# All loads of the modulation weights ahead, the first head in halves, the context last

## The chip, the core and the metric

The kernel runs on one core of one Trainium2 chip. The metric is the device time of one execution in microseconds (us), lower is better. The engines are PE (TensorE, matrix products; PEld is its weight load), DVE (VectorE), ACT (ScalarE), POOL (GpSimd) and SP (SyncE, which here issues nearly all DMAs from one queue in order).

## What is computed

One layer of a diffusion backbone on 1024 latent tokens and 256 context tokens of width 1024, all in float32. Cut to the part that the change touches:

```python
shift, scale, gate = split(silu(c) @ w_mod + b_mod, 3)       # w_mod: 1024 x 3072
hc = rmsnorm(ctx, norm_g) * (1 + scale_c) + shift_c          # the same w_mod, with c_ctx
hx = rmsnorm(x, norm_g) * (1 + scale_x) + shift_x
q, k, v, lr_f, lr_b, ... = split(h @ w_in, ...)              # 4 heads, 128 keys, 256 values
la = log_sigmoid(lr @ w_gate_up + b) / 16                    # a decay per direction
s_f, s_b = final states of the gated linear attention over the context
o = gated linear attention over the latents, both directions, starting from s_f and s_b
```

Behind it come a pooling branch, two sets of gates, two branch projections, an output projection, the residual and a last RMS norm. The change leaves all of these alone.

## The kernel before, in words

Activations are kept transposed, as h^T: eight row tiles of 128 features (kt = 0 to 7; 0 to 3 is the first row half, 4 to 7 the second) by two halves of 512 tokens. To keep float32 accuracy at the faster matrix rate, an operand is split into a rounded part and a rest (`split`, L82: one copy on ACT, one subtraction on DVE), and a product W^T h becomes three products: hi hi, hi lo, lo hi.

The start goes as follows. Small vectors are loaded and turned into columns. **Modulation** (L201 to L236) has four parts b = 0 to 3: shift and scale of the first row half, then shift and scale of the second. Each has eight weight tiles of 128x512 (256 KB, tag `h`, 32 slots). For an even kt the float32 tile is multiplied whole (L214, which the trace shows as two instructions a tile); for an odd one it is split and multiplied twice (L216 to L219). A part ends with a copy of its PSUM row by ACT (tile `on`), four small transposes into bank `po` (L223) and two or three small DVE operations into `shA` or `sA` (L227 to L233). Between the weight tiles the ten token tiles of 512 KB are loaded and normalised (`load_x` and `normalise`, L118 to L133: two squares with sums on ACT, two small DVE operations, a power on POOL, two scalings on DVE): latent tiles 2 to 5 (first token half) during parts 0 and 1, the context's 0 and 1 and latent tiles 6 to 9 (second half) during parts 2 and 3. The low-rank weights are loaded at the start of part 2 (L136, one DMA of 128 KB and eight of 32 KB).

`latent_rows` and `context_rows` (L185, L192) make h^T: PE transposes four (or two) token blocks into a bank, ACT and DVE scale, shift and split it (`split_rows`, L174, banks `sc` and `pj` in turn). First half rows 0 to 3 follow part 1 (L236); the rest comes after part 3 (L594 to L599) in the order: latent rows 4 to 7 of the first token half, low-rank product 1, context rows, low-rank product 0, all rows of the second token half, low-rank product 2. Then `ctx_gates` (L322: decays of the context, through tile `xm` with the one slot of tag `bx`), the first head's keys (`head_k`), the context's keys with the same weights (`ctx_k`), queries (`head_q`), the decays of the latents (`gates`, L448, again in `bx`), values (`head_v`), the context's state for head 0, then for heads 1 to 3 (L608 to L610). After that four times `gla(h)` (scores and states) with the projections of head h + 1.

Program order is a priority and not the order on an engine: a planner places each instruction when, by its own model, its inputs, its slots and its engine are free, and among the ready ones takes the first in program order. Once planned, each engine's queue, SP's too, runs in that order. Every tag has a fixed number of slots (L37) and PSUM banks (L39: `pj` 3, `sc` 2, `o`, `st`, `tr` 1 each); a tile waits for a slot until the last reader of an earlier tile is done. Weights of `w_in` come as 512 KB through `wr` (2 slots) and are split into `wh` and `wl` (4 slots each).

Of the kernel before, what the change touches and what calls it, by code (L numbers as in the profile page):

```python
# [10 lines left out]
F32R = mybir.dt.float32r  # L11
# [4 lines left out]
P = 128  # L16
D = 1024
# [18 lines left out]
# slots of the one SBUF pool, by tag; PSUM banks, by tag  # L36
# [6 lines left out]
def hybrid_kernel(ctx: ExitStack, tc: tile.TileContext, x, ctx_in, rows, w_mod, b_gate_row,  # L43
# [35 lines left out]
    def load(out, in_):  # L79
        return nc.sync.dma_start(out=out, in_=in_)  # L80

    def split(hi, lo, src):  # L82
        """src = hi + lo, exactly, both float32r"""
        act(hi, src)
        tt(lo, src, hi.bitcast(F32), ALU.subtract)
# [4 lines left out]
    # ---- constants and small vectors as columns  # L90
# [20 lines left out]
    # ---- token tiles: load, root mean square, normalise  # L111
# [6 lines left out]
    def load_x(t):  # L118
        tag = "S0" if t < 2 else "v" if t < 6 else "qk"
        loaded.append(t)  # L120
# [14 lines left out]
    # ---- low-rank gate inputs, stacked parts on partitions  # L135
    def low_rank_weights():  # L136
        wraw = T("wr", [P, KT, 32])
# [8 lines left out]
        wup = T("wr", [P, HALF])  # L146
        for rep in range(4):
            load(wup[rep * 16:(rep + 1) * 16], w_up_f)
            load(wup[64 + rep * 16:64 + (rep + 1) * 16], w_up_b)
# [4 lines left out]
    # ---- modulation: shift and scale as columns [d, (latent, context)]  # L154
# [8 lines left out]
    def modulate(kt, t0, n, c, ptag):  # L163
        """psum of one row tile of xn^T and the scale and shift that make it h^T"""
# [9 lines left out]
    def split_rows(kt, t0, n, c, hi, lo):  # L174
        pt, sc_c, sh_c = modulate(kt, t0, n, c, ("sc", "pj")[kt % 2])
# [23 lines left out]
    token_tiles = [2, 3, 4, 5, 0, 1, 6, 7, 8, 9]  # L199
    loaded = []  # L200
    for b in range(4):  # L201
        s_, half_ = b % 2, b // 2
        c0 = s_ * D + half_ * HALF
        pm = PT("st" if b % 2 else "tr")
        if b == 2:
            wlr, wup_hi, wup_lo = low_rank_weights()
        for kt in range(KT):
            w = T("h", [P, HALF])
            load(w, w_mod[kt * P:(kt + 1) * P, c0:c0 + HALF])
            if kt % 2 == 1 and token_tiles and b * KT + kt in (1, 3, 5, 7, 17, 19, 21, 23, 25, 27):  # L210
                load_x(token_tiles.pop(0))
                normalise(loaded[-1])
            if kt % 2 == 0:
                mm(pm[:4], sil4[:, kt, :], w, kt == 0, kt == KT - 1)  # L214
                continue
# [3 lines left out]
            mm(pm[:4], cs4[:, kt, :], lo, False, kt == KT - 1)  # L219
        mrow = T("on", [4, HALF])  # L220
# [14 lines left out]
        if b == 1:  # L235
            latent_rows(0, range(4))  # L236
    for t in token_tiles:
        load_x(t)
    for t in token_tiles:
        normalise(t)  # L240

    # ---- weight stream: slots of 1024 columns, split into exact float32r parts
    ahead = [False]

    def wslot(src, shape, col_scale=None):
        """rows [p, k, n] of a weight; per k: (hi, lo)"""
# [18 lines left out]
    def wquad(w, c0, col_scale=None):  # L265
        """256 columns, all rows"""
# [6 lines left out]
    def proj_t(w, rhs_hi, rhs_lo, n):  # L273
        """psum[128 columns, n tokens] = W^T h"""
# [9 lines left out]
    def proj_n(w, lhs_hi, lhs_lo, tok):  # L284
        """psum[128 tokens, 256 columns] = h W"""
# [33 lines left out]
    # ---- context: final states of both directions  # L319
# [29 lines left out]
    def transpose_k(src, tag):  # L349
        """four of [dk, 128] -> [token, chunk, dk]"""  # L350
# [39 lines left out]
    # ---- latent heads  # L390
# [15 lines left out]
    def head_v(h, st):  # L406
        wv = weights_v(h)
        for t in range(8):
# [21 lines left out]
    # Queries and keys lie with their two decays side by side: slot 1 is what a left block gives to the  # L430
    # scores with its right neighbour (backward decay of queries, forward of keys), slot 0 is for right blocks.
    # Decays of tokens and blocks: array 0 has the backward one of the even and the forward one of the odd,
    # array 1 the others.
# [679 lines left out]
```

## Time and profile before

| what | value |
|---|---|
| device time, median of 3 runs | 1151.29 us (1150.8 to 1152.05) |
| span of the profiled execution | 1152.8 us |
| PE busy | 97% of the span |
| DVE, ACT busy | 70%, 43% |
| mean DMA rate | 120 GB/s |
| chain that ended last | PE 86%, DMA 6%, ACT 2%, DVE 2% |

The profiled execution has no time of its own beside its span; the span is 1.5 us above the median of the runs. The table says which engine is full on average. What the start of the kernel costs doesn't show in it, since the start is a twelfth of the span.

### The profile page before, as it was taken

The page shows a single profiled execution, that of the slowest core. Times are in us where ns is not written, and L with a number is a line of the kernel's source. Part 1 is how long each engine was busy: PE and PEld are TensorE (multiplying, and loading weights), DVE is VectorE, ACT ScalarE, POOL GpSimd, SP SyncE. Part 2 cuts the span into 40 slices and gives each one's busy share as a digit, 9 for nine tenths or more (in the row PEclk, how much of TensorE's full clock was granted, in tenths as well). Part 3 has the DMA queues.
Part 4 walks back from the last instruction along what each step waited for, and adds up shares of the span by engine and source line. Part 5 has one row for each costly group of instructions (what it writes and reads, how often), then busy time and mean ns, then how long its engine had stood idle before and what let it go on. Part 6 is the DMA issues. An engine that isn't in the chain of part 4 may idle for free.

```text
span 1152.8 us, 16292 instructions
## 1 busy us (share of the span) xinstructions
PE 1119.6 (97%) x5993; PEld 926.7 (80%) x5993; DVE 812.2 (70%) x1533; ACT 493.4 (43%) x962; POOL 24.2 (2%) x50
## 2 busy tenths in 40 slices
PE   6799999999999999999999999999999999999997
PEld 1268998798798798788888888888887886878997
DVE  4677458488588587698988867665768776757454
ACT  6697552462452552543333433343446324113233
POOL 0100000000000000100000000000000000000001
PEclk9899999999999999999999999999999999999999
DMA  8812150120220310103251463524448468982113
GB/s 292 291 37 74 42 151 28 56 73 20 65 65 20 85 44 20 55 28 119 82 161 50 128 201 119 167 84 129 151 137 269 161 197 287 298 302 94 38 38 146
DMA packets 119660, 138.40 MB, mean 120 GB/s; under 512 B 8803, under 2 KB 80669, under 8 KB 119454
## 3 DMA queue, kind: packets, MB, share of 16 engines
q1 hardware_dynamic: 119582, 137.38, 37.6%
q8 instruction: 47, 0.77, 0.3%
q14 instruction: 31, 0.25, 0.1%
HBM read 100.65 MB, written 32.51 MB: 116 GB/s over the span
## 4 chain that ended last, share of the span: by engine, by line
PE 86%; DMA 6%; ACT 2%; DVE 2%; issue 2%; SPq 1%; POOL 1%; POOLq 0%; ACTq 0%; DVEq 0%
PE ppj L77 59%; PE psc L77 19%; PE pst L77 3%; PE po L77 2%; DMA h<-w_mod 1%; DMA qk<-ga 1%; PE ptr L77 1%; DMA qk<-x 1%; DMA qk<-gb_T 1%; DMA wr<-w_in 1%; PE ptr L353 1%; ACT sw L63 1%; SPq L80 1%; DMA wr<-w_b 0%; DMA S<-ctx 0%
## 5 line engine op out<-in xcount | busy, mean ns | idle before, releaser
L77 PE MATMUL ppj<-h,wh 128*128 128x512 f32 x794 | 257.9, 401 | 1.0 <-ACT h L63 1.0
L63 ACT ACTIVATE wh<-wr 128x512 fp32r<-128x512 f32 (+1 forms) x183 | 113.7, 627 | 189.9 <-PE ppj L77 108.0
L77 PEld LDWEIGHTS ppj<-h,wh 128*128 128x128 f32 x794 | 146.8, 188 | 35.1 <-issue 2.9
L66 DVE TENSOR_TENSOR wl<-wr,wh 128x512 fp32r<-128x512 f32 (+1 forms) x183 | 124.8, 686 | 61.2 <-ACT wh L63 56.2
L77 PE MATMUL ppj<-wh,h 128*128 128x256 f32 x800 | 157.7, 283 | 0.0
L77 PE MATMUL ppj<-h,wl 128*128 128x512 f32 x397 | 157.2, 396 | 0.0
L77 PEld LDWEIGHTS ppj<-wh,h 128*128 128x128 f32 x800 | 129.9, 190 | 0.5 <-ACT qk L63 0.4
L77 PE MATMUL ppj<-wl,h 128*128 128x256 f32 x400 | 113.2, 283 | 0.0
L77 PEld LDWEIGHTS ppj<-h,wl 128*128 128x128 f32 x397 | 74.6, 188 | 15.1
L77 PEld LDWEIGHTS ppj<-wl,h 128*128 128x128 f32 x400 | 76.0, 190 | 0.2
L77 PEld LDWEIGHTS psc<-z,s 128*128 128x128 f32 x384 | 48.1, 188 | 9.8 <-issue 7.6
L487 DVE COPY_PREDICATED A<-msk,psc 128x512 f32<-128x512 uint8 x56 | 41.2, 735 | 19.8 <-PE psc L77 19.7
L77 PE MATMUL psc<-z,s 128*128 128x128 f32 x384 | 53.5, 280 | 0.0
L63 ACT ACTIVATE s<-s 128x512 f32<-128x512 f32 x60 | 36.9, 629 | 36.7 <-DVE s L66 31.6
L66 DVE TENSOR_TENSOR s<-s,ppj 128x512 f32<-128x512 f32 x60 | 40.7, 683 | 17.0 <-PE ppj L77 17.0
L63 ACT ACTIVATE s<-qk 128x256 f32<-128x256 f32 x56 | 23.1, 420 | 59.8 <-DVE qk L66 59.8
L74 DVE SCALAR_TENSOR_TENSOR S<-S,dec,pst 128x256 f32<-128x256 f32 x56 | 26.8, 478 | 26.3 <-PE pst L77 26.0
L77 PE MATMUL ppj<-S,wh 128*128 128x512 f32 (+1 forms) x132 | 41.2, 371 | 0.0
L77 PE MATMUL psc<-h,wh 128*128 128x512 f32 x126 | 39.1, 392 | 0.0
L66 DVE TENSOR_TENSOR s<-s,psc 128x512 f32<-128x512 f32 x43 | 29.2, 683 | 11.9 <-PE psc L77 10.2
L66 DVE TENSOR_TENSOR s<-s,bx 128x256 f32<-128x256 f32 (+1 forms) x64 | 30.5, 487 | 7.5 <-ACT bx L63 7.5
L66 DVE TENSOR_TENSOR on<-wr,wr 128x512 f32<-128x512 f32 x21 | 14.5, 691 | 30.0 <-DMA wr<-w_in 24.2
(518 smaller groups left out, 2390.3 us busy)
## 6 DMA issues: line engine op xcount, KB each, us to landing
wr<-w_in SPq DMA_DIRECT2D x65, 512.0 KB, 3.9
h<-w_mod SPq DMA_DIRECT2D x32, 256.0 KB, 5.4
qk<-sg SPq DMA_DIRECT2D x32, 256.0 KB, 5.3
sg<-s SPq DMA_DIRECT2D x28, 256.0 KB, 2.1
sw<-qk SPq DMA_DIRECT2D x64, 64.0 KB, 2.0
gb_T<-qk SPq DMA_DIRECT2D x16, 256.0 KB, 3.6
qk<-o SPq DMA_DIRECT2D x16, 256.0 KB, 4.7
ga<-s SPq DMA_DIRECT2D x16, 256.0 KB, 2.2
```

The costliest lines, as they stand in the source:

```text
L63: return nc.scalar.activation(out, in_, func, **kw)
L66: return nc.vector.tensor_tensor(out=out, in0=a, in1=b, op=op)
L74: return nc.vector.scalar_tensor_tensor(out=out, in0=a, scalar=s, in1=b, op0=op0, op1=op1)
L77: return nc.tensor.matmul(out, lhsT=lhsT, rhs=rhs, start=start, stop=stop)
L80: return nc.sync.dma_start(out=out, in_=in_)
L353: nc.tensor.transpose(pt[:, i * P:(i + 1) * P], src[i], ident)
L487: nc.vector.copy_predicated(A, msk[:, li:li + 1, :].to_broadcast([P, CPH, P]), chunks(pl))
```

## The change

All 32 modulation loads are issued ahead of the remaining token tiles, with the first head's key and query weights between them. Token tiles 6 to 9 follow them, and the context's two tiles come last. Parts 0 and 1 split two of eight weight tiles in place of four. The first head's keys and queries are multiplied for the first token half in two pieces, row tiles 0 to 3 and 4 to 7, in banks that stay open between; values of the first token half follow. Then come the second token half's rows, keys, queries and values, and after them the context: rows, low-rank product, keys, `ctx_gates`, and `gates(0)`. The head's key weights lie in the slot of tag `bx`, its query weights in four slots of `s2`. The low-rank up-weights are loaded by two DMAs in place of eight. Rows are made in banks `sc` alone. Comments are dropped too.

```diff
     def load_x(t):
-        tag = "S0" if t < 2 else "v" if t < 6 else "qk"
-        loaded.append(t)
+        tag = "S0" if t < 2 else "v" if t < 6 else "kt" if t == 6 else "S"
         src = ctx_in[t * P:(t + 1) * P] if t < 2 else x[(t - 2) * P:(t - 1) * P]
...
     def low_rank_weights():
-        wraw = T("wr", [P, KT, 32])
+        wraw = T("A", [P, KT, 32])
         load(wraw, w_in[:, O_LR:O_LR + 32].rearrange("(k p) n -> p k n", p=P))
...
-        wup = T("wr", [P, HALF])
-        for rep in range(4):
-            load(wup[rep * 16:(rep + 1) * 16], w_up_f)
-            load(wup[64 + rep * 16:64 + (rep + 1) * 16], w_up_b)
+        wup = T("sw", [P, HALF])
+        for d, src in enumerate((w_up_f, w_up_b)):
+            load(wup[64 * d:64 * d + 64],
+                 src.rearrange("(a r) n -> a r n", a=1).to_broadcast([4, 16, HALF]))
         wup_hi, wup_lo = T("lr", [P, HALF], F32R), T("lr", [P, HALF], F32R)
         split(wup_hi, wup_lo, wup)
...
     def split_rows(kt, t0, n, c, hi, lo):
-        pt, sc_c, sh_c = modulate(kt, t0, n, c, ("sc", "pj")[kt % 2])
+        pt, sc_c, sh_c = modulate(kt, t0, n, c, "sc")
         hf = T("s2", [P, n])
...
-    token_tiles = [2, 3, 4, 5, 0, 1, 6, 7, 8, 9]
-    loaded = []
-    for b in range(4):
-        s_, half_ = b % 2, b // 2
-        c0 = s_ * D + half_ * HALF
-        pm = PT("st" if b % 2 else "tr")
-        if b == 2:
-            wlr, wup_hi, wup_lo = low_rank_weights()
-        for kt in range(KT):
-            w = T("h", [P, HALF])
-            load(w, w_mod[kt * P:(kt + 1) * P, c0:c0 + HALF])
-            if kt % 2 == 1 and token_tiles and b * KT + kt in (1, 3, 5, 7, 17, 19, 21, 23, 25, 27):
-                load_x(token_tiles.pop(0))
-                normalise(loaded[-1])
-            if kt % 2 == 0:
+    def mod_load(b, kts):
+        c0 = (b % 2) * D + (b // 2) * HALF
+        ws = []
+        for kt in kts:
+            ws.append(T("h", [P, HALF]))
+            load(ws[-1], w_mod[kt * P:(kt + 1) * P, c0:c0 + HALF])
+        return ws
+
+    def mod_part(b, pm, ws, kts):
+        for w, kt in zip(ws, kts):
+            if kt % (4, 2)[b // 2] != (3, 1)[b // 2]:
                 mm(pm[:4], sil4[:, kt, :], w, kt == 0, kt == KT - 1)
                 continue
             hi, lo = T("wh", [P, HALF], F32R), T("wl", [P, HALF], F32R)
             split(hi, lo, w)
             mm(pm[:4], cs4[:, kt, :], hi, kt == 0, False)
             mm(pm[:4], cs4[:, kt, :], lo, False, kt == KT - 1)
+
+    def mod_finish(b, pm):
+        s_, half_ = b % 2, b // 2
...
-        if b == 1:
-            latent_rows(0, range(4))
-    for t in token_tiles:
-        load_x(t)
-    for t in token_tiles:
-        normalise(t)
+    x_after = {(0, 3): 2, (0, 7): 3, (1, 1): 4, (1, 4): 5}
+    for b in range(2):
+        pm = PT("st" if b % 2 else "tr")
+        for kt in range(KT):
+            ws = mod_load(b, [kt])
+            if (b, kt) in x_after:
+                load_x(x_after[b, kt])
+                normalise(x_after[b, kt])
+            mod_part(b, pm, ws, [kt])
+        mod_finish(b, pm)
...
-    def head_v(h, st):
-        wv = weights_v(h)
-        for t in range(8):
+    def head_v(h, st, hf=None, wv=None):
+        wv = wv or weights_v(h)
+        for t in range(8) if hf is None else range(hf * CPH, hf * CPH + CPH):
...
-    msk_f = T("bx", [P, len(LEVELS), P])
-    load(msk_f, masks)
-    nc.vector.tensor_copy(msk, msk_f)
+
+    def head_weights(c0, tiles):
+        raw = T("wr", [P, KT, P])
+        load(raw, wcols(w_in, c0))
+
+        def go():
+            for i in range(2):
+                split(*tiles[i], raw[:, 4 * i:4 * i + 4, :])
+            return [tuple(t[:, k, :] for t in tiles[i]) for i in range(2) for k in range(4)]
+        return go
+
+    def proj_part(pt, w, hf, kts):
+        for k in kts:
+            whi, wlo = w[k]
+            mm(pt, whi, hH[hf][k], k == 0, False)
+            mm(pt, whi, hL[hf][k], False, False)
+            mm(pt, wlo, hH[hf][k], False, k == KT - 1)
+
+    st = new_head()
+    kbig = T("bx", [P, 2, KT, P], F32R)
+    k_go = head_weights(O_K, [(kbig[:, 0, 4 * i:4 * i + 4], kbig[:, 1, 4 * i:4 * i + 4]) for i in range(2)])
+    ws2 = mod_load(2, range(KT))
+    q_go = head_weights(O_Q, [(T("s2", [P, 4, P], F32R), T("s2", [P, 4, P], F32R)) for i in range(2)])
+    ws3 = mod_load(3, range(KT))
+    wlr, wup_hi, wup_lo = low_rank_weights()
+    latent_rows(0, range(4))
+    pm2, pm3 = PT("tr"), PT("st")
+    mod_part(2, pm2, ws2[:4], range(4))
+    wk = k_go()
+    mod_part(2, pm2, ws2[4:], range(4, KT))
+    pk, pq = PT("pj"), PT("pj")
+    proj_part(pk, wk, 0, range(4))
+    mod_finish(2, pm2)
+    mod_part(3, pm3, ws3[:4], range(4))
+    wq = q_go()
+    mod_part(3, pm3, ws3[4:], range(4, KT))
+    mod_finish(3, pm3)
+    proj_part(pq, wq, 0, range(4))
+    for t in (6, 7, 8, 9):
+        load_x(t)
+    latent_rows(0, range(4, KT))
+    proj_part(pk, wk, 0, range(4, KT))
     rope_t = T("t8", [P, 2, L])
     load(rope_t, rope)
     cosT, sinT = rope_t[:, 0, :], rope_t[:, 1, :]
-    latent_rows(0, range(4, KT))
+    proj_part(pq, wq, 0, range(4, KT))
+    for t in (6, 7):
+        normalise(t)
+    st["k"][0] = rope_apply(pk, 0, 1.0)
+    wv = weights_v(0)
+    for t in (8, 9):
+        normalise(t)
+    st["q"][0] = rope_apply(pq, 0, float(P) ** -0.5)
+    head_v(0, st, 0, wv)
     low_rank(1, hH[0], hL[0])
+    latent_rows(1, range(0, KT))
+    for t in (0, 1):
+        load_x(t)
+    msk_f = T("z", [P, L + 2 * PAD])[:, :len(LEVELS) * P]
+    load(msk_f, masks.rearrange("p a b -> p (a b)"))
+    pk, pq = PT("pj"), PT("pj")
+    proj_part(pk, wk, 1, range(KT))
+    st["k"][1] = rope_apply(pk, 1, 1.0)
+    proj_part(pq, wq, 1, range(KT))
+    st["q"][1] = rope_apply(pq, 1, float(P) ** -0.5)
+    low_rank(2, hH[1], hL[1])
+    for t in (0, 1):
+        normalise(t)
+    head_v(0, st, 1, wv)
     context_rows()
     low_rank(0, hcH, hcL)
-    latent_rows(1, range(0, KT))
-    low_rank(2, hH[1], hL[1])
+    kc = ctx_k(wk)
     e_ctx = ctx_gates()
-    st = new_head()
-    wk = head_k(0, st)
-    kc = ctx_k(wk)
-    head_q(0, st)
+    nc.vector.tensor_copy(msk, chunks(msk_f))
     decays = gates(0)
-    wv = head_v(0, st)
     ctx_state(0, kc, ctx_v(wv))
```

## Rows read from the trace of the kernel before

**Rows 1.** The page, busy time of each engine over the whole span.
```profile
span 1152.8 us, 16292 instructions
PE 1119.6 (97%) x5993; PEld 926.7 (80%) x5993; DVE 812.2 (70%) x1533; ACT 493.4 (43%) x962; POOL 24.2 (2%) x50
```

**Rows 2.** Stretches: start:end, length, busy by engine (instructions), granted clock, DMA share, GB/s.
```profile
0.00:25.00 25.00, 17.97 (x57) 4.28 (x57) 10.77 (x30) 14.31 (x35) 2.53 (x9) 1.00 0.85 288
25.00:55.00 30.00, 20.53 (x64) 6.56 (x64) 18.21 (x48) 20.01 (x49) 3.29 (x6) 0.89 0.91 320
55.00:74.00 19.00, 16.83 (x87) 11.83 (x88) 17.61 (x33) 18.02 (x36) 0.00 (x0) 0.91 0.16 42
74.00:91.00 17.00, 16.88 (x71) 11.89 (x70) 11.34 (x25) 13.55 (x22) 0.10 (x1) 1.00 0.11 31
91.00:165.00 74.00, 73.75 (x544) 69.82 (x543) 42.65 (x97) 44.60 (x79) 0.10 (x1) 1.00 0.30 83
165.00:1152.80 987.80, 973.65 (x5177) 822.34 (x5175) 711.58 (x1302) 382.90 (x746) 18.23 (x33) 1.00 0.37 116
```

**Rows 3.** Instruction groups of PE, 0 to 90.9 us, three of 22.
```profile
L77 PE MATMUL ppj<-h,z 128*128 128x512 f32 x32 | 11.6, 468 | 1.7 <-ACT h L63 1.5 <-DVE h L66 0.2
L77 PE MATMUL ppj<-h,wh 128*128 128x512 f32 x32 | 11.4, 413 | 0.0
L77 PE MATMUL ptr<-h,sil 128*4 128x512 f32 x16 | 10.7, 759 | 2.4 <-ACT sil L63 2.4
```

**Rows 4.** The chain that ended last: start, length, engine and work.
```profile
66.25 0.44 PE psc L167 x4
73.25 0.43 PE po L77 x2
93.66 11.15 PE ppj L77 x50
105.93 29.16 PE ppj L77 x240
```

**Rows 5.** PE in order of time: start, length, work, [idle before, releaser].
```profile
20.20 1.02 PE L77 MATMUL pst<-h,sil 128*4 128x512 f32 x2
21.16 0.39 PE L77 MATMUL pst<-wh,cs 128*4 128x512 f32 x1
25.47 0.41 PE L223 MATMUL po<-cst,on 4*128 4x4 f32 x4 [0.68 <-ACT on L63]
...
38.96 1.87 PE L77 MATMUL ptr<-h,sil 128*4 128x512 f32 x2
...
53.27 0.41 PE L223 MATMUL po<-cst,on 4*128 4x4 f32 x4 [0.68 <-ACT on L63]
```

**Rows 6.** DMA view, 0 to 60 us, 40 slices of 1.5 us.
```profile
GB/s 0 145 299 320 275 272 403 407 393 389 382 389 388 327 142 79 307 273 359 347 406 380 396 389 389 384 396 374 395 418 421 362 296 254 44 0 0 0 0 0
```

**Rows 7.** ACT in order of time: first product split after the last load of part 1.
```profile
21.84 0.63 ACT L63 ACTIVATE wh<-h 128x512 fp32r<-128x512 f32 x1 [0.93 <-DMA h<-w_mod]
```

**Rows 8.** The chain that ended last, from the last modulation load on.
```profile
39.39 4.33 DMA h<-w_mod
43.73 0.61 ACT wh L63
...
48.58 0.56 POOL rstd L131
...
54.31 0.79 ACT h L63
```

**Rows 9.** From the context's rows to the first head's scores: PE, ACT and DVE in order of time.
```profile
55.81 0.48 PE L167 MATMUL ppj<-cst,S 128*128 128x128 f32 x1
...
70.04 0.50 PE L77 MATMUL po<-lr,lr 64*128 64x256 f32 x2
...
123.64 1.90 ACT L63 ACTIVATE bx<-bx 128x2032 f32<-128x2032 f32 x1 [2.12 <-DVE bx L66]
...
169.80 0.69 DVE L74 SCALAR_TENSOR_TENSOR A<-psc,cst 128x512 f32<-128x512 f32 x1
```

## The prediction, made before the change was run

> **What bounds the kernel now.** I read the page first: PE is busy for 97% of the span, no other engine for more than 70% [rows 1]. Then the stretches: from 91 us to the end PE is busy for 73.75 of 74.0 and 973.65 of 987.8 us, so it idles for 14 us in 1062 [rows 2]. From there on, whatever PE has done earlier comes off the end. Before 91 us PE looks busy as well, but its busy time misleads: it counts latencies and products at the lower clock. So I count its work instead, at the spacing that products show when they follow each other closely [rows 3 to 5]: 0.223 us for 512 columns (50 in 11.15 us), 0.1215 for 256 (240 in 29.16), 0.11 for a transpose, 0.215 for a gate product, 0.96 for a float32 modulation tile multiplied whole (20.20 to 21.16).
>
> By 90.9 us PE has done: 16 whole tiles 15.4; 32 products of split tiles 7.1; 32 low-rank products on latents 7.1 and 16 on context 1.9; 48 of the first keys 10.7; 80 transposes 8.8; 18 gate products 3.9; four ends of modulation parts 1.6. That is 56.5 us, so **34.4 of the first 90.9 us are lost to PE**. Of them 11.5 fall before 25 us (8 whole tiles, 16 products, 16 transposes and one end are 13.5). The other 22.9 come after it, and the chain says where: loads run at 380 to 400 GB/s [rows 6] and the last modulation tile lands at 43.7, but the first row that needs it starts at 54.3, since two tiles' normalisation, with a power on POOL in each, stands among the last splits on the in-order ACT and DVE [rows 8]. Then, from 55 to 74 us, DVE and ACT are busy for 17.6 and 18.0 of 19 us making rows [rows 2], while PE has only transposes and low-rank products. The first head, PE's bulk, begins at 74.
>
> **The change, part by part.** I ask when PE will have done the same work. Parts 0 and 1 multiply four more tiles whole and eight products fewer: +3.8 − 1.8 = +2.1 us (rounded), so the list is 58.6. The rest is the time that PE still loses, each term with both ends.
>
> a) Up to 25 us. Loads of parts 0 and 1 and tiles 2 to 5 are the same bytes, so the end of part 1 (25.47, [rows 5]) stays. The 2.1 us of more work fall partly into waits for loads. PE loses 11.5 now; I take 10 (10 to 12).
>
> b) Start of part 2. Its loads follow at once, PE has them while ACT and DVE make rows 0 to 3. 1 (0 to 2).
>
> c) End of part 3. Part 1's last tile landed at 21.8 [rows 7]. Behind it come the key weights, part 2, the query weights and part 3: 0.52 + 2.10 + 0.52 + 2.10 = 5.24 MB at 390 GB/s, 13.4 us, so part 3's last tile lands at 35.3, 8.4 us earlier than now. From the last load to the first row part 1 needs 4.7 us (21.84 to 25.47, and 1.04 more as from 53.27 to 54.31), part 3 now 10.6 (43.7 to 54.3) [rows 5, 7, 8]. With the normalisations behind it I expect the shorter way, so rows 4 to 7 start near 41. PE has 18.5 us to do between 25 and there: the two parts 11.3, 16 transposes 1.8, first pieces of keys and queries 5.4. It is covered nearly throughout. If the planner again puts tiles 6 to 9 among the last splits, ACT waits there for loads that land at 41 to 44. 3 (1 to 6).
>
> d) Values. Tiles 6 to 9, the rope table and the value weights are 4.2 MB behind part 3: 10.8 us, about 46 and with the low-rank loads 49; 53 if the context and the masks (1.5 MB) pass the value weights, which wait for both `wr` slots on SP with the rope exchanges queued behind them. PE's cover from 44.5 is the second pieces of keys and queries (5.4) and low-rank product 1 (3.6), to 53.5. 2 (0 to 4).
>
> The low-rank weights cause a dip to 142 and 79 GB/s at 19.5 to 24 us, worth 3.2 us of full rate [rows 6]. The change moves it behind part 3 and issues three DMAs for nine; I count 3 us before tiles 6 to 9, inside d. The Trainium skill (DMA: Bandwidth & Descriptors, Specifications) gives 512 bytes as the least transfer for line rate; the 128-byte rows of this load lie below it and the dip agrees. By it the dip would move whole and d would be 4: 1140 in place of 1138.
>
> e) Rows of the second token half. The same ACT and DVE work as now at 55 to 74, but PE has 23.3 us of values beside it, half of them without those rows. One pair of banks `sc` in place of five banks costs nothing while PE has that cover; without it I'd count 2 to 3 us. 2 (0 to 5).
>
> f) The context. Its rows, products and states move whole behind the head; PE has other work, so only hand-overs are lost. The key weights keep the `bx` slot until `ctx_k`; behind it wait `ctx_gates` and then `gates(0)` on ACT and DVE, and PE's scores wait for those. 1 (0 to 6; the far case is a rival).
>
> Everything else (the rope exchanges of the head's first half, earlier on SP; the mask's cast; the powers of four tiles on POOL) lies beside this cover and counts nothing; without it four powers at 0.56 us [rows 8] are 2.2 us.
>
> **Sum:** 10 + 1 + 3 + 2 + 2 + 1 = 19 us lost, with ends of 11 and 35. 58.6 + 19 = 77.6 us against 90.9: 13.3 us gained. The span goes from 1152.8 to 1139.5; the median of the runs is 1.5 us below the span, so **1138.0 us**. The ends give 1130 and 1154.
>
> **Rivals.** A measurement of this kernel tells 0.2%, 2.3 us, from no change.
>
> *All covered.* PE finds work at every hand-over: losses of 13, a gain of 19.3, 1132 us. For it: from 25 us on PE nearly always has two independent streams. Against: queues in order, planned on modelled times.
>
> *The lower clock.* The granted clock is 0.89 from 25 to 55 us and 0.91 from 55 to 74 [rows 2], and after 38 us a pair that takes 1.02 us takes 1.87 [rows 5], which is 1.2 for 2.4 GHz, in a stretch where PE is busy for 20.5 of 30 us. If half of the 18.5 to 19.4 us of work between 25 and 45 runs so, 9.5 us go: 1147.5. Against it: PE has less to wait for there. The Trainium skill (TensorE: Matmul & The Clock Gate, HAM oscillation) says that waits for loads between short groups of products make each group start at the low clock; the 1.87 us agree, and the loads still pace this stretch.
>
> *The context's chain ends up slower.* PE passes the values of the second half at 85 us of work (24.6 modulation, 1.6, 7.0, 7.1, 21.4 keys and queries, 23.3 values) plus 18 lost: 103. If the planner leaves the context's transposes till then, the chain from the first of them to the end of `gates(0)`, 55.81 to 125.54 now, 69.7 us [rows 9], ends at 173. PE's own work until then is 49 us, to 152: transposes 1.8, low-rank 1.9, gates 5.2, and for each of four heads keys 2.9, values 5.8 and a state 1.4. 20 us are open, which outweighs the gain: 1158. It decides once the gap exceeds 13 us and nothing fills it. Against it: head 1's projections (96 products of 512 columns and 192 of 256, 44.7 us) need nothing of that chain, the context's tiles are there at some 55 us, and scores on DVE start at 169.8 now, 44 us after the decays were ready [rows 9].
>
> *It doesn't do what it says.* The planner sorts by readiness and takes program order only among what is ready, so the queues may end up much as they are: 1151.
>
> **How the numbers follow.** Forecast 0.52, all covered 0.20, lower clock 0.10, context's chain 0.10, nothing 0.08. Faster by over 0.2% (below 1149): the first two and 0.07 of the third, 0.79. Within: 0.03 + 0.08 = 0.11. Slower: 0.10. The range 1129 to 1150 holds the first three, 0.82.
>
> **What would show it.** In the changed profile: the last modulation tile lands near 35 us and rows 4 to 7 start near 41 (c); the first product with value weights at 49 to 54 (d); PE idle below 3 us between 45 and 100; a granted clock of 1.00 from 25 us on, against the clock's rival. The first keys, low-rank products and both gates done would be 13 us earlier than at 90.9, and everything behind, such as the first scores' DVE operation at 169.8, earlier by about as much. Wrong I'd be if that operation isn't earlier while PE's products are: then the chain through `bx` bounds, and the gain is given back there.

## The result and the profile after

The changed kernel takes 1165.16 us, the median of 4 runs (1162.57 to 1168.17), beside 1151.67 us for the kernel before in 4 runs on the same chip. The ratio is 1.0111, with a 95% interval of 1.009 to 1.0133: **slower by 1.1%**, where 1.2% faster was forecast. The profiled execution is the slowest of the four: 1168.17 us, with a span of 1166.4.

The page of the kernel after, where [rows 1] show the kernel before:

```profile
span 1166.4 us, 16240 instructions
PE 1124.1 (96%) x5993; PEld 931.0 (80%) x5993; DVE 809.8 (69%) x1529; ACT 491.8 (42%) x958; POOL 24.2 (2%) x50
```

PE has as many instructions as before and is busy for 4.5 us more, while the span is 13.6 us longer. So most of the loss is time in which PE stands. The stretches of [rows 2], read again in the kernel after (start:end, length, busy by engine, granted clock, DMA share, GB/s), say where:

```profile
0.00:25.00 25.00, 18.59 (x51) 4.02 (x51) 9.12 (x27) 12.40 (x29) 2.53 (x9) 1.00 0.94 328
25.00:55.00 30.00, 20.83 (x64) 7.63 (x65) 15.17 (x35) 17.41 (x41) 1.65 (x3) 0.77 0.97 306
55.00:74.00 19.00, 18.63 (x121) 16.28 (x120) 11.85 (x30) 11.31 (x26) 1.64 (x3) 1.00 0.35 101
74.00:91.00 17.00, 15.72 (x95) 13.23 (x94) 11.01 (x16) 9.67 (x16) 0.00 (x0) 1.00 0.03 8
91.00:165.00 74.00, 66.36 (x447) 58.79 (x445) 39.75 (x81) 44.26 (x78) 0.20 (x2) 0.98 0.20 55
165.00:1166.00 1001.00, 984.00 (x5222) 831.04 (x5220) 722.92 (x1344) 396.79 (x771) 18.22 (x33) 1.00 0.36 115
```

In two places this isn't what was forecast. From 25 to 55 us PE is as little busy as before and its clock is 0.77 (0.89 before). From 91 to 165 us, where it idled for 0.25 us, it now idles for 7.6. From 55 to 74 us it is better: 121 instructions in place of 87.

Busy time counts waits for latency and the low clock as work, so I count PE's lost time as the prediction did: the length of a stretch less its instructions at full-rate spacing (0.223 us for 512 columns, 0.1215 for 256, 0.11 a transpose, 0.22 a gate product, 0.48 for each of the two instructions of a whole tile, 0.10 a small transpose). The stretches are cut at fixed times, and the runs that follow stand beside it. An instruction that lies across a cut counts on both sides, so that a count can come out a little below zero; it is good to about 1 us, and what is read from it is differences between kernels.

```
us lost to PE       0-25  25-55  55-74  74-113  113-200    sum
before              10.9   13.9    6.7     1.2      4.7   37.4
after                8.8   14.4    0.8     2.0     20.5   46.5
e1                   9.6   13.0    0.8     8.1     10.5   42.0
e2                   9.8    7.7    0.2     2.6     20.3   40.6
e3                  10.9   13.7    5.1    -0.6     23.4   52.5
e4                   9.2   10.1    0.7     2.7     21.7   44.4
e6                   9.7    6.2    6.2     2.9      9.3   34.3
e7                  10.9   12.7    9.6     2.8      4.7   40.7
e8                   8.9   14.0    0.9     1.9     12.2   37.9
e11                 10.9   13.0    4.2     3.3     11.6   42.9
```

The column 113-200, and with it the sum, is some 3 us too high in every row: products of the states (`pst<-S,on`, 256 columns) are counted at 0.1215 us, and follow each other in the trace at 0.215 (eight of them take 1.99 us). The differences stay.

To 200 us the change loses 46.5 − 37.4 = 9.1 us more, and does 2.1 us more work for its whole tiles: 11.2 us together. DVE's score operations show that this is nearly all of it. Its timeline before (the first such operation, at 169.80, is in [rows 9]) and after:

```profile
172.62 0.73 DVE L487 COPY_PREDICATED A<-msk,psc 128x512 f32<-128x512 uint8 x1 [2.13 <-PE psc L77]
...
190.38 0.68 DVE L74 SCALAR_TENSOR_TENSOR A<-psc,cst 128x512 f32<-128x512 f32 x1
```

```profile
158.86 0.68 DVE L74 SCALAR_TENSOR_TENSOR A<-psc,cst 128x512 f32<-128x512 f32 x1
...
182.26 0.73 DVE L490 COPY_PREDICATED A<-msk,psc 128x512 f32<-128x512 uint8 x1
...
200.45 0.68 DVE L74 SCALAR_TENSOR_TENSOR A<-psc,cst 128x512 f32<-128x512 f32 x1
```

The first score operation, which the prediction had named as its sign, comes 10.9 us earlier (158.86). It doesn't wait for the decays: it is done before `gates(0)` ends, at 179.9. The first masked one behind it (`COPY_PREDICATED`) starts 2.4 us after that end, where it started 47 us after it before, and it is 9.6 us later than before. The second score operation is 10.1 us later, the third goes from 255.50 to 266.65 (11.1 later), and POOL's memset of a tile `z` from 641.94 to 653.26 (11.3):

```profile
641.94 0.96 POOL L916 MEMSET z<- 128x1024 f32 x1 [57.36 <-DVE z L66]
```

```profile
653.26 0.96 POOL L974 MEMSET z<- 128x1024 f32 x1 [57.84 <-DVE z L66]
```

So most of the time is lost before some 200 us, and nearly nothing between there and 642. The last 2.3 us of the 13.6 come behind that: from 880 to 910 us the granted clock is 0.89 here, and 1.00 in the same work before (868.7 to 898.7). Of the traces below some have such a dip near 900 us and some don't. Of the two sides, up to 113 us the change wins 32.7 − 26.0 = 6.7 us, and from 113 to 200 it gives back 15.8.

**From 113 to 200 us.** What PE waits for there, in the view of its waits in the kernel after, 91 to 200 us (total, times, longest):

```profile
PE psc L77 <- DVE s L71: 3.4, 1, 3.4
PE pst L77 <- ACT on L63: 2.7, 2, 1.6
PE ppj L77 <- ACT S L63: 2.3, 1, 2.3
PE po L77 <- DVE bx L71: 0.9, 1, 0.9
```

At all four PE waits for ACT or DVE, for a step of one chain or for a copy (`S`, `on`) that stands behind such steps in ACT's queue. ACT's timeline shows the chain from end to end: the context's first row, a table load (`ACT_TABLE_LOAD`), the context's decays (`z`), the first decay of `gates(0)`, and its last exponential:

```profile
112.97 0.56 ACT L63 ACTIVATE S<-psc,shA,sA 128x256 fp32r<-128x256 f32 x1
...
129.55 1.28 ACT L63 ACT_TABLE_LOAD   x1
130.84 1.06 ACT L63 ACTIVATE z<-z 128x1024 f32<-128x1024 f32 x1
...
154.28 0.85 ACT L63 ACTIVATE bx<-psc,cols 128x256 f32<-128x256 f32 x2 [2.99 <-DVE z L319]
...
178.00 1.91 ACT L63 ACTIVATE bx<-bx 128x2032 f32<-128x2032 f32 x1 [0.83 <-DVE bx L66]
```

From 113.0 to 179.9 it takes 67 us (67.4 from the first transpose, at 112.5), against 69.7 before, from the first transpose at 55.8 to 125.5 [rows 9]. Seven table loads of 1.28 us stand in it on ACT in both kernels, 9 us of the 67. The chain is about as long as it was and begins 57 us later. What differs is what PE has beside it. The chain that ended last shows that it passes through ACT's and DVE's queues, among the splits of the context weights of other heads (the same view, 142 to 154 us):

```profile
142.04 0.36 ACT kt L63
142.41 0.52 ACT wh L63
142.93 0.36 ACT z L63
143.29 0.52 ACT wh L63
143.81 0.95 ACT z L63
...
151.41 0.69 DVE wl L66
152.10 2.16 DVE z L319 x6
```

**From 25 to 58 us.** The same view at the start, up to the last of part 3's products:

```profile
24.95 6.53 DMA h<-w_mod
...
32.24 8.75 DMA sw<-w_up_b
...
41.08 0.64 ACT lr L63
...
43.09 6.47 PE ptr L77 x13
...
51.31 3.57 PE pst L77 x10
```

ACT's timeline there:

```profile
41.08 0.63 ACT L63 ACTIVATE lr<-sw 128x512 fp32r<-128x512 f32 x1 [1.62 <-DMA sw<-w_up_b]
41.61 2.69 ACT L63 ACTIVATE wh<-h 128x512 fp32r<-128x512 f32 x5
...
57.71 0.78 ACT L63 ACTIVATE h<-psc,shA,sA 128x512 fp32r<-128x512 f32 x1
```

And PE's:

```profile
30.85 1.87 PE L77 MATMUL pst<-h,sil 128*4 128x512 f32 x2 [5.86 <-DMA h<-w_mod]
...
42.28 0.40 PE L77 MATMUL ptr<-wh,cs 128*4 128x512 f32 x1 [2.91 <-ACT wh L63]
```

Part 3's last load is issued at 30.15 us and lands 5.7 us later, at 35.9, so the weights are there when forecast (35.3). But ACT has the copy of the low-rank up-weights, which land at 41.0, ahead of the splits of parts 2 and 3, and five of these run in one go behind it. Before that, PE stands 5.86 us for a tile of part 3 that the planner put ahead of the rows' transposes, and ACT stands 6.43 us, to 34.34, for these transposes. Rows 4 to 7 start at 57.7 us: later than the 54.3 of before [rows 8], not earlier.

In the kernel before, the last load of part 3 is issued at 40.06 and lands at 45.7, not at 43.7 as the prediction read from [rows 8]. The split that starts at 43.7 had waited behind a copy of ACT, and this copy for PE, which was still at part 2:

```profile
43.24 0.59 ACT L63 ACTIVATE on<-ptr 4x512 f32<-4x512 f32 x1 [4.55 <-PE ptr L77]
```

### The profile page after: what moved, and what is told of

Its sections match the earlier page's. It is cut to its first block, busy times and chain, and to the rows that moved or that the text cites. A ratio compares the mean times of both kernels' runs of the same rounds, so it can differ in the third digit from the quotient of the medians.

```text
span 1166.4 us, 16240 instructions
## 1 busy us (share of the span) xinstructions
PE 1124.1 (96%) x5993; PEld 931.0 (80%) x5993; DVE 809.8 (69%) x1529; ACT 491.8 (42%) x958; POOL 24.2 (2%) x50
## 3 DMA queue, kind: packets, MB, share of 16 engines
q1 hardware_dynamic: 119462, 137.38, 36.9%
## 4 chain that ended last, share of the span: by engine, by line
PE 85%; DMA 6%; ACT 4%; DVE 2%; issue 1%; POOL 1%; SPq 0%; POOLq 0%; ACTq 0%; DVEq 0%
PE ppj L77 58%; PE psc L77 19%; PE pst L77 3%; PE po L77 2%; PE ptr L77 2%; DMA h<-w_mod 2%; DMA qk<-ga 1%; DMA qk<-gb_T 1%; DMA v<-x 1%; DMA sw<-w_up_b 1%; PE ptr L356 1%; ACT L63 1%; ACT wh L63 1%; DVE wl L66 1%; DMA wr<-w_b 0%
## 5 line engine op out<-in xcount | busy, mean ns | idle before, releaser
L77 PE MATMUL ppj<-h,wh 128*128 128x512 f32 x730 | 237.1, 401 | 1.0 <-ACT h L63 0.8
L63 ACT ACTIVATE wh<-wr 128x512 fp32r<-128x512 f32 x178 | 109.9, 627 | 191.3 <-PE ppj L77 121.4
L77 PEld LDWEIGHTS ppj<-h,wh 128*128 128x128 f32 x730 | 135.0, 188 | 32.5 <-issue 2.6
L66 DVE TENSOR_TENSOR wl<-wr,wh 128x512 fp32r<-128x512 f32 x178 | 120.8, 686 | 46.3 <-ACT wh L63 38.9
L77 PE MATMUL ppj<-h,wl 128*128 128x512 f32 x365 | 145.1, 398 | 0.0
L77 PEld LDWEIGHTS ppj<-h,wl 128*128 128x128 f32 x365 | 68.6, 188 | 14.0 <-issue 0.4
L63 ACT ACTIVATE s<-s 128x512 f32<-128x512 f32 x60 | 36.9, 629 | 34.5 <-DVE s L66 31.3
L77 PE MATMUL ppj<-S,wh 128*128 128x512 f32 (+1 forms) x124 | 38.3, 371 | 0.0
L66 DVE TENSOR_TENSOR on<-wr,wr 128x512 f32<-128x512 f32 x21 | 14.5, 690 | 29.3 <-DMA wr<-w_in 23.7
```

The lines of the kernel that those rows point to most:

```text
L63: return nc.scalar.activation(out, in_, func, **kw)
L66: return nc.vector.tensor_tensor(out=out, in0=a, in1=b, op=op)
L77: return nc.tensor.matmul(out, lhsT=lhsT, rhs=rhs, start=start, stop=stop)
```

## The experiments

Ratios are to the kernel before, run on the same chip, with the 95% interval; as the median of the kernel before lies between 1151.67 and 1153.79 us from one group of runs to the next, two experiments are compared by their ratios (0.1% is 1.15 us). Each edit is to the kernel after, except where the heading names before, e3 or e6. Of the edits the lines that matter are shown; `...` marks what is left out.

**e1, the context ahead of the second half's keys.** If the gap from 113 us on is the chain without cover, an earlier chain with the second half's values beside it closes it.

```diff
+    for t in (0, 1):
+        normalise(t)
+    context_rows()
+    low_rank(0, hcH, hcL)
     pk, pq = PT("pj"), PT("pj")
...
-    for t in (0, 1):
-        normalise(t)
-    head_v(0, st, 1, wv)
-    context_rows()
-    low_rank(0, hcH, hcL)
...
     decays = gates(0)
+    head_v(0, st, 1, wv)
     ctx_state(0, kc, ctx_v(wv))
```

> The changed kernel with the context's rows and low-rank product put before the second token half's keys, and that half's values after both gates. Theory 1 (the chain from the context's rows through its gates to gates(0) starts too late, at 113 us, and PE runs out of other work between 136 and 177): PE loses under 5 us between 91 and 200 in place of some 15, the second score operation of DVE (200.45 in the changed kernel, 190.38 before) comes at 187 to 192, time 1150 to 1156. Theory 2 (all of the loss is made before 58 us, by queues that stand behind late loads): no difference over 3 us, 1162 to 1166. A third theory, that the lower clock of the first 55 us and the more whole products cost it: 1162 to 1166 too.

Measured: 1162.75 us, 1.0093 (1.0076 to 1.0109). The loss from 113 to 200 us falls from 20.5 to 10.5, but from 74 to 113 it rises from 2.0 to 8.1: the cover that the values give late is missing early. The second score operation comes at 197.57 us, 2.9 earlier. The time lies in the range set for the other theories and not in that of the chain; what speaks for the chain is where the loss moved. The gap follows the cover, and the sum of the cover is what seems short.

**e2, the low-rank weights ahead of part 2.** If ACT's copy of the up-weights blocks the splits behind it, loading them first moves rows 4 to 7.

```diff
     st = new_head()
+    wlr, wup_hi, wup_lo = low_rank_weights()
     kbig = T("bx", [P, 2, KT, P], F32R)
...
     ws3 = mod_load(3, range(KT))
-    wlr, wup_hi, wup_lo = low_rank_weights()
     latent_rows(0, range(4))
```

> The changed kernel with the low-rank weights loaded and split ahead of the key weights and of part 2, as before, so that ACT doesn't wait for their load (landed at 41.0 us) in front of the splits of parts 2 and 3. Theory 2: rows 4 to 7 start at 46 to 50 us in place of 57.7, and everything behind comes 8 to 11 us earlier, 1154 to 1158. Theory 1: the rows come earlier by the same, but the chain through the context decides later, so that half of it or more is kept only if PE reaches the context earlier too: 1156 to 1163. The clock alone: 1163 to 1166.

Measured: 1161.84 us, 1.009 (1.0071 to 1.0109). ACT's timeline in this kernel:

```profile
26.45 0.63 ACT L63 ACTIVATE lr<-sw 128x512 fp32r<-128x512 f32 x1 [0.69 <-DMA sw<-w_up_b]
29.25 0.63 ACT L63 ACTIVATE wh<-h 128x512 fp32r<-128x512 f32 x1 [0.20 <-DMA h<-w_mod]
...
50.73 0.78 ACT L63 ACTIVATE h<-psc,shA,sA 128x512 fp32r<-128x512 f32 x1
```

The splits start at 29.3 in place of 41.6 and rows 4 to 7 at 50.7 in place of 57.7. The loss up to 113 us falls by 5.7; the one from 113 on stays (20.3). In the trace the place of the low-rank weights (three loads of 128 KB, their splits and copies, which the edit moves together) is worth some 5 us; the granted clock from 25 to 55 us rises from 0.77 to 0.94 with it, so part of that may be the clock's. By the ratios it is 0.2%, and the two intervals overlap.

**e3, the kernel before with the context last.** Nothing of the change but its end: the start, the loads and the heads' pieces stay as before.

```diff
-    token_tiles = [2, 3, 4, 5, 0, 1, 6, 7, 8, 9]
+    token_tiles = [2, 3, 4, 5, 6, 7, 8, 9, 0, 1]
...
+    head_k(0, st)
+    head_q(0, st)
+    head_v(0, st)
     context_rows()
     low_rank(0, hcH, hcL)
...
     e_ctx = ctx_gates()
...
     decays = gates(0)
...
     ahead[0] = True
-    for h in range(1, NH):
+    for h in range(NH):
```

> The kernel before with the context alone moved last: its tiles loaded behind tiles 6 to 9, its rows, low-rank product and gates after the first head's values, gates(0) after them; head 0's context products load their weights again, as heads 1 to 3 do (1.5 MB and six splits more). Theory 1: it loses 10 to 20 us against the kernel before, between 110 and 200 us, 1161 to 1171. Theory 2 and the clock: within 3 us of before, 1149 to 1155.

Measured: 1169.33 us, 1.0156 (1.0137 to 1.0175), slower than the whole change. The loss from 113 to 200 us goes from 4.7 to 23.4. Head 0's context weights are loaded and split a second time here, so the pure price of the order is taken from its pair:

**e11, e3 with the values behind.** One line moves: `head_v(0, st)` goes behind `gates(0)`.

```diff
-    head_v(0, st)
     context_rows()
     low_rank(0, hcH, hcL)
     e_ctx = ctx_gates()
     decays = gates(0)
+    head_v(0, st)
```

> The kernel before with the context last, as in the run that lost 17 us, but with the first head's values (23.3 us of PE) behind the context's gates and gates(0) instead of ahead of the context. Theory of the cover: PE's loss between 113 and 200 us falls from 23 us to under 10, and the ratio from 1.0156 to 1.003 to 1.008. If the late loads of the context's tiles or its weights loaded twice cost it: 1.012 or more.

Measured: 1159.87 us, 1.0047 (1.003 to 1.0065), in the range of the cover. The loss from 113 to 200 us falls from 23.4 to 11.6 (under 10 was expected). The stretches show it, e3 first, then e11 (columns as above):

```profile
140.00:160.00 20.00, 11.35 (x71) 9.71 (x71) 15.77 (x36) 16.75 (x28) 0.10 (x1) 0.88 0.36 105
```

```profile
140.00:160.00 20.00, 18.73 (x137) 17.77 (x138) 16.87 (x49) 15.98 (x33) 0.00 (x0) 1.00 0.42 122
```

ACT and DVE have the same 16 to 17 us of 20 in both. With the values behind it PE gets through 137 instructions beside them, without them 71. The same work in the same kernel, moved behind the chain in program order, is worth 1.1% of the time, 12.6 us; the loss that goes is 11.8.

**e4, the slot of `bx`.** The rival for the gap: `ctx_gates` and `gates(0)` share one slot, and the second waits for the first.

```diff
-        xm = T("bx", [P, 2, 2, 2, LC])
-        xm = [xm[:, i] for i in range(2)]
+        xm = [T("qk", [P, 2, LC]) for _ in range(NH)]
...
     kc = ctx_k(wk)
+    decays = gates(0)
     e_ctx = ctx_gates()
     nc.vector.tensor_copy(msk, chunks(msk_f))
-    decays = gates(0)
```

> The changed kernel with the tile xm of the context's gates in four slots of tag qk, so that gates(0) waits for the key weights' slot alone and not for the context's scans; gates(0) stands before them in the program. Theory 1, in the form that the slot bx makes the chain: gates(0) starts near 122 us in place of 154, PE loses under 6 us between 113 and 200, time 1152 to 1158. If the chain's length comes from the order on ACT and DVE and not from the slot: 1160 to 1166. Theory 2: 1162 to 1166.

Measured: 1167.81 us, 1.0142 (1.0114 to 1.017): no better than the change, and above every range that was set. `gates(0)` does start earlier, at 119.4 us, and ends at 148.2, 32 us earlier than in the change; but the first masked operation starts at 180.7, only 1.6 earlier. The loss from 113 on is 21.7 and has only moved, to the other gates. The stretch from 160 us in this kernel, which before had PE busy all along:

```profile
160.00:180.00 20.00, 13.54 (x69) 11.16 (x69) 14.11 (x30) 14.59 (x29) 0.10 (x1) 0.74 0.07 20
```

So the slot sets when `gates(0)` comes, and isn't what costs the time. Whichever gates come first, those of the other kind follow on the same two engines.

**e5, e1 and e2 together.** Both diffs above.

> Both edits at once: low-rank weights early, and the context's rows, gates and gates(0) ahead of the second half's values. If the two losses are separate (queues behind late loads until 58 us; first-head products used up before the chain through the context needs cover), the gains of 5 to 6 and 3 to 4 us add: the time is 1154 to 1157. If both edits buy the same microseconds: 1159 to 1163.

Measured: 1159.94 us, 1.0063 (1.0042 to 1.0083): 0.48% under the change, where the two alone gave 0.18% and 0.21%. The time itself falls into the range set for one common loss, since that of the sum was set from gains of 3 to 6 us each, and each alone brought about 2. The traces add up: the second score operation comes 7.8 us earlier than in the change (192.66), against 2.9 and 5.4 for the two alone. So start and end are, within the intervals, separate losses.

**e6, the changed start with the order of before behind it.** Loads first, the first head's keys and queries in halves, low-rank weights early; then the context's rows, the second half's rows, keys, `ctx_gates`, queries, `gates(0)` and all values as before. The tile `xm` has the slots of e4.

```diff
+    wlr, wup_hi, wup_lo = low_rank_weights()
     kbig = T("bx", [P, 2, KT, P], F32R)
...
+    context_rows()
+    low_rank(0, hcH, hcL)
     wv = weights_v(0)
...
     e_ctx = ctx_gates()
+    proj_part(pq, wq, 1, range(KT))
+    st["q"][1] = rope_apply(pq, 1, float(P) ** -0.5)
     decays = gates(0)
+    head_v(0, st, 0, wv)
+    head_v(0, st, 1, wv)
     ctx_state(0, kc, ctx_v(wv))
```

> The changed start (modulation loads ahead, first keys and queries in two pieces, low-rank weights early) with the context's tiles, rows, gates and gates(0) in the order of before, the first head's values and second-half keys and queries left as PE's work beside them; the context's gates use slots of qk. Theory of the cover (the chain rows, low-rank products, context gates, gates(0) takes about 70 us of ACT and DVE whatever PE does, and the first head's products are what PE has beside it): the chain starts some 5 us earlier than before, PE idles under 6 us between 60 and 180, 1144 to 1152, at least 10 us better than the change. Theory that the early start itself costs the time (clock, queues behind loads): 1158 or more.

Measured: 1157.59 us, 1.0041 (1.0024 to 1.0057): 0.7% under the change, some 8 us, and still not level with before; it lies between the two ranges that were set. Its trace loses 34.3 us to 200 us, 3.1 fewer than before, and does 2.1 more work; the second score operation comes at 189.39 us, 1.0 earlier than before. So even with the chain covered and the queue unblocked the new start brings no more than about 1 us in the trace, and nothing in the medians. It isn't the clock that holds it back: from 25 to 55 us it is granted at 0.94 here and in e2 (e2 first), above the 0.89 of before [rows 2].

```profile
25.00:55.00 30.00, 24.59 (x98) 10.52 (x98) 19.18 (x44) 22.24 (x47) 2.19 (x4) 0.94 1.00 347
```

```profile
25.00:55.00 30.00, 26.13 (x102) 11.90 (x103) 18.98 (x42) 21.82 (x46) 2.19 (x4) 0.94 0.98 342
```

**e10, e6 with the low-rank weights late.** The half of e6 that belongs to the order alone.

```diff
-    wlr, wup_hi, wup_lo = low_rank_weights()
     kbig = T("bx", [P, 2, KT, P], F32R)
...
     ws3 = mod_load(3, range(KT))
+    wlr, wup_hi, wup_lo = low_rank_weights()
```

> The changed kernel with the old order of context, second-half rows and gates alone; the low-rank weights stay behind part 3, as the change has them. Theory of the cover: PE loses under 10 us between 113 and 200 us (20.5 in the change, 4.7 before) and the time is 1.004 to 1.007 of before, most of the way back. Theory of the queues behind late loads as the main cause: 1.008 to 1.011.

Measured: 1162.84 us, 1.0076 (1.0052 to 1.0099), between the two ranges that were set. The old order halves the loss from 113 to 200 us, to some 10.5, and raises the one from 74 to 113 to some 6.5. Rows 4 to 7 start at 57.50 us again, and 25 to 55 us lose 14.2. The late low-rank weights cost 0.35% against e6, 4 us, and 8 us of PE's time in that stretch, which agrees with e2 in kind; the intervals overlap slightly.

**e7, the kernel before with the modulation loads ahead of the token tiles.** Only the load order: in the program the six token tiles of the context and of the second half no longer stand between the tiles of parts 2 and 3. In the trace SP still issues the context's two from 23.15 us on, ahead of both parts (22.72 before); what moves is tiles 6 to 9.

```diff
-            if kt % 2 == 1 and token_tiles and b * KT + kt in (1, 3, 5, 7, 17, 19, 21, 23, 25, 27):
+            if kt % 2 == 1 and token_tiles and b * KT + kt in (1, 3, 5, 7):
```

> The kernel before with one part of the change alone: the six token tiles that stand between the loads of modulation parts 2 and 3 come behind them; nothing else. By the prediction's step c the last modulation tile lands at 36 to 39 us and rows 4 to 7 start at 42 to 46 in place of 54.3, with 5 to 8 us gained: 1143 to 1147. If the rows of context and second half only wait for their own tiles then, on ACT and DVE, which are full from 55 to 74 us: within 3 us of before, 1149 to 1155. If ACT's and PE's queues again stand behind late loads: 1155 to 1160.

Measured: 1157.2 us, 1.0039 (1.0024 to 1.0055). Here rows 4 to 7 do start earlier, at 51.05 us (54.31 before), and it is still slower. ACT's timeline suggests why: the normalisation (squares `A<-qk`) now stands between the rows. The chain that ended last passes through the same tiles on the other engines, with three powers on POOL and six scalings on DVE between 51.5 and 59.2 us.

```profile
51.05 0.78 ACT L63 ACTIVATE h<-psc,shA,sA 128x512 fp32r<-128x512 f32 x1
51.72 0.62 ACT L63 ACTIVATE A<-qk 128x512 f32<-128x512 f32 x1
...
53.00 0.62 ACT L63 ACTIVATE A<-qk 128x512 f32<-128x512 f32 x1
...
54.13 0.62 ACT L63 ACTIVATE A<-qk 128x512 f32<-128x512 f32 x1
```

And the stretch behind it, to be read beside the third of [rows 2]:

```profile
55.00:74.00 19.00, 13.89 (x72) 10.86 (x71) 17.01 (x35) 15.40 (x33) 0.85 (x2) 0.68 0.09 27
```

PE does 72 instructions in place of 87 there, at a clock of 0.68 in place of 0.91. The waits for loads in the kernel before weren't empty: ACT and DVE normalised in them.

**e8, head 1 as cover.** Keys and queries of head 1 go ahead of the context products of heads 1 to 3.

```diff
     ahead[0] = True
+    st1 = new_head()
+    head_k(1, st1)
+    head_q(1, st1)
     for h in range(1, NH):
         ctx_state(h, ctx_k(weights_k(h)), ctx_v(weights_v(h)))
```

> The changed kernel with head 1's keys and queries (96 products of 512 columns, 21.4 us of PE) ahead of the context's heads 1 to 3 in the program. Theory of the cover: PE's idle time between 113 and 180 falls from 10 us to under 4, and what it costs comes back only where the scores of head 0 then lack cover: 1156 to 1163. If ACT and DVE themselves are the limit between 113 and 180, or the loads of weights, then no gain: 1163 to 1170.

Measured: 1162.52 us, 1.0087 (1.0068 to 1.0106). The loss from 113 to 200 us falls by 8.3, to 12.2, but POOL's memset of `z` comes at 651.22 us, only 2.0 earlier than in the change. Counted from 200 to 420 us PE loses 39.6 us in place of 33.7, so 5.9 are given back behind the gap: these products were to cover the first head's scores. The prediction named them as what fills the gap for nothing; they do fill it, and are missing later.

**e12 and e9, the whole tiles.** Parts 0 and 1 split four of eight tiles, as before, in the change (e12) and in e6 (e9).

```diff
-            if kt % (4, 2)[b // 2] != (3, 1)[b // 2]:
+            if kt % 2 == 0:
```

> The change itself with four of eight tiles split in parts 0 and 1, as before. If the whole tiles cost 2.1 us: ratio 1.008 to 1.010 in place of 1.011. If not: 1.010 to 1.013.

> The changed start with the old order of context and gates and early low-rank weights, and now parts 0 and 1 of the modulation split four of eight tiles again, as before (PE has 2.1 us less to do, ACT and DVE two splits more a part). If the whole tiles cost their 2.1 us: about 2 us better than without this edit, ratio 1.001 to 1.003. If they fall into PE's waits for loads: no difference, 1.003 to 1.006.

Measured: e12 1166.8 us, 1.0109 (1.0083 to 1.0135); e9 1156.87 us, 1.0034 (1.0015 to 1.0052). Neither can be told from its pair; in both traces POOL's memset of `z` comes 2.1 us later than in the pair. The 2.1 us of additional product time cost nothing that shows: without them PE loses 12.4 us (e12) in place of 8.8 up to 25 us, waiting for the same loads.

## Why the prediction was wrong

The frame held. PE's lost time to 200 us plus its additional work gives the shift (11.2 us worked out, 10.1 to 11.3 read). The terms did not.

- **f, the context, is the step that failed: "1 (0 to 6)", measured 15.8.** It was costed at hand-overs, since "PE has other work". That work was never listed against the chain's length. The prediction's own rival did it: a chain of 69.7 us, 49 us of PE work beside it, 20 open. Measured were a chain of 67 us and a loss of 20.5 in the same count (some 17 with the states' products at their spacing). Its 1158 was too low by 7, because it took the gains of the other terms as given. It had a chance of 0.10 on two grounds. One was that scores start "44 us after the decays were ready". But the operation read there, at 169.8, doesn't wait for the decays: in the changed kernel it comes 10.9 us earlier while everything behind `gates(0)` comes later, so it couldn't be the sign of failure that the prediction made of it either. The other ground was that head 1's projections fill the gap. The changed program has the context products of heads 1 to 3 ahead of them; and e8, which puts head 1's keys and queries in front (21.4 of the 44.7 us), gets 8.3 us in the gap and pays 5.9 later. The pair e3 and e11 shows the cause in the kernel before, without any other part of the change.
- **b and c, part 2 to rows 4 to 7: "1 (0 to 2)" and "3 (1 to 6)", measured 14.4 us in 25 to 55.** The loads came as forecast (35.9, forecast 35.3); the rows came at 57.7, not near 41. Two assumptions failed. First, the rival trap was named for tiles 6 to 9 ("ACT waits there for loads that land at 41 to 44"), and what stood there was the low-rank weights, which the prediction had put down as 3 us of DMA time inside d: a load's place on the consumer's queue cost more than its bytes (e2: 5.7 us, the clock's part in it included). Second, the shorter way from the last load to the first row was taken to be free of the normalisation; in e7 this work, taken out of the loads' shadow, lands between the rows. In e2, e6 and e7 rows 4 to 7 start at 50.4 to 51.1, never near 41.
- **a: 10, measured 8.8; d and e: 4 together, measured 2.8 from 55 to 113.** These held. The first product with value weights starts at 58.00 rather than 49 to 54, and PE has keys and queries until then: from 45 to 100 us it idles for 1.65 us, where under 3 was forecast.
- **The whole tiles, +2.1 us.** Right as work, but free in time (e12).
- **The lower clock** was a rival at 0.10. The granted clock did fall, to 0.77 from 25 to 55 us, in stretches in which PE stands for loads or for ACT (5.86 and 2.91 us above). In e2 and e6 it is 0.94 there, above the 0.89 of before, and both are still slower than before; so it isn't the main cause. What it costs in the change itself no run sets apart; it is counted here inside b and c.

Put together: 16.4 us were to be won up to the end of the head, and 1 to be lost at the context. 6.7 were won, 2.1 us of work added, and 15.8 lost.

**Still open.** e6 has a trace level with before (POOL's memset of `z` at 642.15 against 641.94 us, spans of 1152.4 and 1152.8), and a median 0.4% longer. Its profiled execution is the fastest of its seven (1154.16, median 1157.59). Profiled executions of the runs here take about 1.8 us more than their span; if that holds for the one of before, it took some 1154.6, about 3 more than the 1151.29 of its runs. Runs of one kernel lie up to 8 us apart (e9: 1152.78 to 1160.78), and this goes along with the granted clock: of the 34 runs of before beside e1 to e12, the two at a mean clock of 0.990 took 1156.4 and 1156.6 us, the eight at 0.996 took 1149.4 to 1153.8. The trace of e6 is one at 0.996, that of before at 0.995, so comparing the two flatters e6. Where in e6 the 0.4% lie isn't known. No version tried is faster than the kernel before.

## What to carry to other kernels

Before the bounding engine's work is pulled forward, list what it lay beside: a chain over other engines keeps about its length (69.7 and 67 us here; 63 to 77 in the runs other than e4, from the context's first row on ACT to the end of `gates(0)`), and it needs about as much independent work in program order behind its start as it is long. A wait for loads on the bounding engine is worth removing only as far as the other engines have nothing to do in it. And where engines run planned queues in order, ask of each load which instruction consumes it, and what stands behind that one: three loads of 128 KB were worth some 5 us there, in the trace of e2.

## What the runs showed of the hardware

The two DMAs that load the up-weights, each a source of 16 rows repeated four times into 64 partitions, 128 KB on the destination's side, were not short: the last took 8.75 us from issue to landing in the change, and the DMA view of 0 to 60 us (40 slices of 1.5 us) has 220 to 243 GB/s in the four slices from 34.5 us on, where it had 372 to 389 in the three before:

```profile
GB/s 0 138 295 325 303 363 388 406 402 391 385 388 388 339 321 382 388 385 327 332 389 385 372 230 220 243 243 359 322 382 379 272 94 236 389 351 78 0 43 304
```

The 128-byte rows of the low-rank weights, which stood in the slices of 142 and 79 GB/s before [rows 6], are loaded in the same stretch. They have landed by 36.9 us, when ACT's first split of them starts, and the two slices from 37.5 us on still have 243 GB/s; so they aren't the whole of it, and what makes the up-weights slow no run shows:

```profile
36.92 0.42 ACT L63 ACTIVATE wh<-A 128x256 fp32r<-128x256 f32 x1 [0.95 <-DMA A<-w_in]
```

The Trainium skill (DMA: Bandwidth & Descriptors, Specifications) gives 512 bytes as the least transfer for line rate. The 142 and 79 GB/s agree with it for the low-rank weights; the rows of the up-weights, 2 KB each, are longer than that and took 8.75 us all the same.
